# Six gate tiles of an encoder layer as two by two block products with seven blocks (Strassen), on one core

## The chip, the cores and the metric

The kernel runs on one core of a Trainium2 chip. The metric is the device time of one execution in microseconds (us). Before the change it is 935.38 us, the median of 3 runs (935.34 to 936.16 us). The profile is one execution, and TensorE was granted its full clock in it from 6.5 us to 931.5 us.

## What is computed

One layer of an encoder on 512 tokens of width 1024: three token mixers side by side (neighbourhood attention, grouped-query attention, attention to 256 memory tokens), each projected and weighted by a gate, then an output projection, a layer norm, a mixture of 16 experts in which each expert picks its 64 tokens, and a second layer norm.

```python
z = jnp.einsum('bsd,df->bsf', x, w_in[l])
q_na, k_na, v_na, q_g, k_g, v_g, q_m, gate_logits = jnp.split(z, _split_points(), axis=-1)
...
branches = jnp.stack([y_na, y_gqa, y_mem], axis=2)
proj = jnp.einsum('bsgk,gkd->bsgd', branches, w_branch[l])
gates = jax.nn.sigmoid(gate_logits + b_gate[l]).reshape(B, S, N_BRANCH, D)
merged = jnp.sum(gates * proj, axis=2)
mix = jnp.einsum('bsd,de->bse', merged, w_out[l])
x = layer_norm(DN_ALPHA * x + mix, ln1_g[l], ln1_b[l])
ffn = expert_choice_ffn(x, w_router[l], w_gate_up[l], w_down[l])
x = layer_norm(DN_ALPHA * x + ffn, ln2_g[l], ln2_b[l])
```

The gates are the part that the change touches: `gate_logits` has 3 x 1024 columns, 24 tiles of 128, eight for each branch.

## The kernel before

**Products in three passes.** Ahead of the experts every float32 operand is split into two parts of the type fp32r. `hi_lo` does this: a cast on ScalarE (`hi`), then a subtraction on VectorE (`lo`). A product is hi·hi + hi·lo + lo·hi, three instructions of TensorE (L306 to L308). The layer's input stands in SBUF as `xh` and `xl`, each in two halves (`a`, `b`) of 4 chunks x 512 tokens.

**Weight units.** The weights ahead of the experts are 74 units of 512 KB (128 x 1024), which `Stream` loads on SyncE's queue (L194), in two places `raw` by turns, and splits two units ahead of their use. A unit of a gate is 8 chunks of 128 columns: `gate_piece` takes one unit and makes 8 x 3 products of 128x512 into one PSUM bank of `mm` (3 banks), and ScalarE evacuates it with a tanh. Units 36 and 37 are the first two gate tiles of branch 1, unit 38 is the weight of its first projection, and 54 to 61 are the eight gate tiles of branch 0.

**Order.** Each engine carries out its instructions in the order in which the program gives them. Memory attention comes first, then the queries, keys and values of the second branch, `g_branch(2)` (gates and projections of the third input), the values of the neighbourhood attention (`g_na_v`), the bias table of its first two heads (`na_bias(0)`: 16 loads on SyncE and 6 sums on GpSimd), its queries and keys (`g_na_qk(0)`), and `g_branch(1)`, whose steps alternate with units of neighbourhood attention (`at.step`). In `between(jp)` the next two heads' bias, queries and keys follow. Then `g_na_gates` makes the eight gate tiles of branch 0, `g_na_proj` projects them, the output projection (`wo`) and the router follow, and the experts end the kernel. Small pieces of work (`bg`) are given out one at each step.

**The experts' weights.** They are 192 units of 1 MB (`gu` and `dn`), streamed by `Ring` through 24 places. The places are SBUF tiles which the mixers used before; `RING` is the order in which they are filled, `ring.more(7)` gives out the first loads behind certain weight units (`after`), and from the experts on each unit that has been read makes room for the next. The products of the experts are L1384 and L1433.

## Time and profile before

| what | value |
|---|---|
| median of 3 runs | 935.38 us |
| the profiled execution | 935.73 us |
| its span, first to last instruction | 934.0 us |
| TensorE busy | 917.7 us, 98% |
| VectorE busy | 452.5 us, 48% |
| ScalarE busy | 280.9 us, 30% |
| GpSimd busy | 71.9 us, 8% |
| queue 1 of the DMAs | 250.22 MB, 67.0% of 16 engines' span |

Times in the rows count from the span's start. PE is TensorE, PEld its weight loads, DVE VectorE, ACT ScalarE, POOL GpSimd, SP SyncE (its DMA queue is SPq). Products are pipelined: the second number of a row of TensorE is longer than the pace, and the pace is read from the distances of the starts. A row names the line, the operation, the tile written and those read, the shapes and how many instructions it stands for; behind it, in brackets, is the idle time of the engine before it and what ended it.

### The profile page before, as it was taken

How to read it: one execution, taken by the hardware profiler on the slowest of the kernel's cores; microseconds unless marked ns; L12 is line 12 of the kernel's file. 1: busy time of each engine (PE TensorE's matmuls, PEld its weight loads, DVE VectorE, ACT ScalarE, POOL GpSimd, SP SyncE). 2: the span in 40 equal slices, each digit the busy share in tenths (PEclk: the TensorE clock that was granted, in tenths of full speed). 3: DMA queues.
4: the chain of work that ended last, by engine and by line, in shares of the span. 5: the costliest groups of instructions: out<-in, count | busy, mean ns of one | idle time of the engine just before them, and what ended most of it. 6: DMA issues, size and time to landing. Idle time of an engine off the chain costs nothing.

```text
span 934.0 us, 13436 instructions
## 1 busy us (share of the span) xinstructions
PE 917.7 (98%) x5501; PEld 604.7 (65%) x5501; DVE 452.5 (48%) x858; ACT 280.9 (30%) x572; POOL 71.9 (8%) x107
## 2 busy tenths in 40 slices
PE   9999999999999999999999999999999999999996
PEld 8899988888888888888787344444343444543332
DVE  6447869875375576326445147223141323422246
ACT  6334443644344454334333011101011011301021
POOL 0100000000122230107023000000000000000001
PEclk9999999999999999999999999999999999999999
DMA  9322221221333332574879999999999999999996
GB/s 366 103 76 64 82 68 46 69 76 60 96 84 115 106 85 72 181 279 176 318 313 360 415 426 432 428 441 425 434 432 433 425 430 429 429 433 428 431 425 275
DMA packets 39868, 251.42 MB, mean 269 GB/s; under 512 B 12704, under 2 KB 13248, under 8 KB 24576
## 3 DMA queue, kind: packets, MB, share of 16 engines
q1 hardware_dynamic: 39584, 250.22, 67.0%
q8 instruction: 43, 0.70, 0.3%
q0 software_dynamic: 80, 0.26, 0.1%
q14 instruction: 17, 0.14, 0.0%
q10 hardware_dynamic: 144, 0.10, 0.0%
HBM read 247.42 MB, written 2.36 MB: 267 GB/s over the span
## 4 chain that ended last, share of the span: by engine, by line
PE 72%; DMA 20%; DVE 4%; ACT 2%; issue 1%; SPq 0%; POOLq 0%; POOL 0%; DVEq 0%; ACTq 0%
DMA dn<-in_wst 11%; DMA gu<-in_wst 8%; PE g L1384 7%; PE u L1384 6%; PE y L1433 6%; PE gate L306 5%; PE gate L308 4%; PE gate L307 4%; PE pr L306 2%; PE pr L307 2%; PE pr L308 2%; PE ga L1350 2%; PE gy L691 2%; PE nqk L308 2%; PE nqk L307 2%; PE nqk L306 2%
## 5 line engine op out<-in xcount | busy, mean ns | idle before, releaser
L1384 PE MATMUL g<-gu,xs 128*64 128x512 f32 x408 | 106.0, 598 | 1.1 <-DMA gu<-in_wst 1.0
L1384 PE MATMUL u<-gu,xs 128*64 128x512 f32 x408 | 104.9, 592 | 0.0
L1433 PE MATMUL y<-dn,hT 128*64 128x512 f32 x376 | 83.6, 593 | 0.9 <-DMA dn<-in_wst 0.8
L150 DVE TENSOR_TENSOR y<-y,y 64x512 fp32r<-64x512 f32 x28 | 19.3, 688 | 120.2 <-ACT y L149 120.2
L150 DVE TENSOR_TENSOR lo_twin<-raw_twin,whi 128x1024 fp32r<-128x1024 f32 x40 | 49.5, 1238 | 45.8 <-ACT whi L149 45.7
L149 ACT CAST y<-y 64x512 fp32r<-64x512 f32 x28 | 16.2, 580 | 174.1 <-PE y L1433 146.6
L1384 PEld LDWEIGHTS u<-gu,xs 128*64 128x64 f32 x408 | 29.4, 137 | 58.1 <-issue 57.6
L149 ACT CAST whi<-raw_twin 128x1024 fp32r<-128x1024 f32 x60 | 63.0, 1050 | 12.1 <-PE wo L1159 9.5
L1433 PEld LDWEIGHTS y<-dn,hT 128*64 128x64 f32 x376 | 27.0, 137 | 54.5 <-issue 51.2
L1384 PEld LDWEIGHTS g<-gu,xs 128*64 128x64 f32 x408 | 26.8, 137 | 46.6 <-issue 39.4
L1417 DVE COPY hT<-ht 128x512 f32<-128x512 f32 x15 | 10.4, 692 | 61.3 <-PE ht L1414 61.3
L306 PE MATMUL gate<-xha,whi 128*128 128x512 f32 x96 | 38.7, 403 | 0.0
L307 PE MATMUL gate<-xla,whi 128*128 128x512 f32 x96 | 37.4, 390 | 0.0
L306 PE MATMUL gate<-xhb,whi 128*128 128x512 f32 x96 | 37.3, 389 | 0.0
L307 PE MATMUL gate<-xlb,whi 128*128 128x512 f32 x96 | 37.3, 389 | 0.0
L712 POOL TENSOR_TENSOR bm<-bf,hm 128x256 f32<-128x256 f32 x24 | 17.9, 785 | 235.4 <-DMA bf<-in_rpb 231.5
L1521 DVE TENSOR_TENSOR acc<-acc,cb 128x512 f32<-128x512 f32 x56 | 34.0, 681 | 3.7 <-PE cb L1519 3.7
L1350 PEld LDWEIGHTS <-x 128*128 128x128 f16 (+1 forms) x576 | 29.7, 100 | 9.0 <-issue 8.7
L1405 DVE SCALAR_TENSOR_TENSOR h<-h,g 128x512 f32<-128x512 f32 x16 | 11.0, 687 | 50.0 <-ACT h L1404 50.0
L665 ACT ACTIVATE P_twin<-gs,nm 128x512 f32<-128x512 f32 x32 | 21.7, 684 | 42.8 <-DVE nm L664 42.8
L150 DVE TENSOR_TENSOR wlo<-raw_twin,whi 128x1024 fp32r<-128x1024 f32 x20 | 25.2, 1258 | 18.0 <-ACT whi L149 17.9
L308 PE MATMUL gate<-xha,lo_twin 128*128 128x512 f32 x80 | 31.2, 391 | 0.0
(481 smaller groups left out, 2000.5 us busy)
## 6 DMA issues: line engine op xcount, KB each, us to landing
gu<-in_wst SPq DMA_DIRECT2D x31, 2048.0 KB
gu<-in_wst SPq DMA_DIRECT2D x45, 1024.0 KB
raw_twin<-in_wu SPq DMA_DIRECT2D x65, 512.0 KB
dn<-in_wst SPq DMA_DIRECT2D x15, 2048.0 KB
dn<-in_wst SPq DMA_DIRECT2D x16, 1024.0 KB
gu<-in_wst SPq DMA_DIRECT2D x4, 4096.0 KB
dn<-in_wst SPq DMA_DIRECT2D x4, 4096.0 KB
gu<-in_wst SPq DMA_DIRECT2D x2, 3072.0 KB
```

Of the source, the lines that this page charges most:

```text
L149: nc.scalar.copy(hi, src)
L150: nc.vector.tensor_tensor(lo, src, hi.bitcast(F32), op=ALU.subtract)
L306: nc.tensor.matmul(acc, w_h, rh[:, k], start=(k == 0), stop=False)
L307: nc.tensor.matmul(acc, w_h, rl[:, k], start=False, stop=False)
L308: nc.tensor.matmul(acc, w_l, rh[:, k], start=False, stop=(k == nk - 1))
L665: nc.scalar.activation(self.p[:, h], self.s[h], AF.Exp, bias=nm[:, h:h + 1], accum_out=self.sm[:, h:h + 1])
L691: nc.tensor.matmul(self.y[h * 64:h * 64 + 64, j * P:(j + 1) * P], ST["vg"][:, kc, kvh * 64:kvh * 64 + 64], u.pt[:, h, kc], start=(kc == 0) ...
L712: nc.gpsimd.tensor_tensor(bm[:, h, ty].rearrange("p (b r c) -> p r b c", b=4, r=8), bf[:, h, :, 16 - 8 * ty:48 - 8 * ty].rearrange("p r (b ...
L1350: nc.tensor.matmul(g[r], part(i, m)[:, f * P + r.start:f * P + r.stop], oh[:, m], start=(i == 0 and m == 0), stop=(i == 1 and m == NT - 1))
L1384: nc.tensor.matmul(GU[e][b][hf * 64:hf * 64 + 64], xs, w[b][:, hf * 512:hf * 512 + 512], start=(k == 0), stop=(k == KD - 1))
L1433: nc.tensor.matmul(ys[o][o * 64:o * 64 + 64], hT[:, c, hf * 64:hf * 64 + 64], w[j][:, o * 512:(o + 1) * 512], start=(first and k == 0 and ...
L1521: nc.vector.tensor_tensor(a, a, cb, op=ALU.add)
```

## The change

Of the eight gate tiles of branch 0 the first two stay as they are. The other six are made as three couples. A couple's weights are a two by two matrix of blocks (two tiles, two halves of the inner dimension) and the input another (two halves of the inner dimension, two halves of the tokens); the product is made of seven block products and sums, each block being 4 chunks x 3 products of 128x256. The sums of the input's quarters (t1 to t4) are made once: x is loaded a second time (`load_x_again`), GpSimd subtracts (`mix_sum`, `mix_raw`), ScalarE casts and GpSimd subtracts the low halves (`mix_split`); t4 goes into a quarter of `xh` and `xl` (`mix_last`). Each couple's weights are summed on GpSimd and VectorE, and four of their sums or blocks are split (`Couple`). `g_couple` makes the seven blocks in two PSUM banks, with copies of the first results on ScalarE and sums on VectorE and GpSimd. The order of the places in the ring is another one, the first expert loads go out two units later, `router_scale` is given out in two parts and, with the rest of the router's preparation, nine steps later, `na_bias` of the next heads stands ahead of the attention steps, and the gates' results lie in other tiles.

```diff
-RING = ("E0", "A2", "A3", "A0", "A1", "B0", "B1", "A8", "P", "PT", "A4", "raw", "VS", "A5", "A6", "G0a", "G0b", "G1a", "lo", "X",
+RING = ("P", "PT", "B1", "E0", "A4", "A2", "A3", "A0", "B0", "A1", "A5", "A6", "A8", "VS", "raw", "G0a", "G0b", "G1a", "lo", "X",
...
-WIDTHS = ((0, 1), (N_SINGLE, 2), (N_PAIR, 4), (112, 2), (182, 1))
+WIDTHS = ((0, 1), (N_SINGLE, 2), (N_PAIR, 4), (112, 2), (181, 1))
...
+COUPLES = range(56, 62, 2)
...
+            self.stop = self.limit = COUPLES[0]
...
+            elif i - i % 2 in COUPLES[::2]:
+                if i % 2 == 0:
+                    self.wide = R("B1", [P, 2, 1024], f"raw{i}")
                 t = self.wide[:, i % 2]
...
-            while self.ns < min(N_UNITS, self.used + n):
+            while self.ns < min(self.stop, self.used + n):
                 self._split()
-            while self.nd < min(N_UNITS, self.ns + self.AHEAD_DMA):
+            self.ahead()
+
+        def ahead(self):
+            while self.nd < min(self.limit, self.ns + self.AHEAD_DMA):
...
+    def quarter(t, c):
+        return t[:, :, c * 256:c * 256 + 256]
+    mixed = {}
+    xq = []
+    def load_x_again():
+        for h in range(2):
+            xq.append(R(("A5", "A6")[h], [P, 4, S], f"xq{h}"))
+            nc.sync.dma_start(xq[h], xt[:, 4 * h:4 * h + 4])
+    def mix_sum(*which):
+        x11, x12, x21, x22 = (quarter(xq[h], c) for h in range(2) for c in range(2))
+        if 1 in which:
+            t12 = R("A7", [P, 2, 4, 256], "mix12")
+            mixed["sums"] = {1: t12[:, 0], 2: t12[:, 1], 3: x12}
+        t = mixed["sums"]
+        for i, a, b in ((1, x12, x11), (2, x22, t[1]), (3, x22, x12)):
+            if i in which:
+                nc.gpsimd.tensor_tensor(t[i], a, b, op=ALU.subtract)
+    def mix_split(*which):
+        for i in which:
+            t = mixed["sums"][i]
+            both = R(("E0", "A4", "A7")[i - 1], [P, 2, 4, 256], f"mx{i}", F32R)
+            mixed[f"t{i}"] = both[:, 0], both[:, 1]
+            nc.scalar.copy(both[:, 0], t)
+            nc.gpsimd.tensor_tensor(both[:, 1], t, both[:, 0].bitcast(F32), op=ALU.subtract)
+    def mix_raw():
+        ST["kept"] = R("A1", [P, 2048], "kept")
+        t4 = ST["kept"][:, :1024].rearrange("p (k c) -> p k c", k=4)
+        x21 = [quarter(x.t[1], 0).bitcast(F32) for x in (xh, xl)]
+        t2 = [t.bitcast(F32) for t in mixed["t2"]]
+        nc.gpsimd.tensor_tensor(t4, x21[0], t2[0], op=ALU.subtract)
+        nc.gpsimd.tensor_tensor(t4, t4, x21[1], op=ALU.add)
+        nc.gpsimd.tensor_tensor(t4, t4, t2[1], op=ALU.subtract)
+        mixed["raw4"] = t4
+    def mix_last():
+        mixed["t4"] = quarter(xh.t[0], 1), quarter(xl.t[0], 1)
+        hi_lo(*mixed["t4"], mixed.pop("raw4"))
+        mixed["x11"] = quarter(xh.t[0], 0), quarter(xl.t[0], 0)
+        for c in range(2):
+            mixed[f"x2{c + 1}"] = quarter(xh.t[1], c), quarter(xl.t[1], c)
+    class Couple:
+        def __init__(self, p):
+            self.p = p
+            ws.ahead()
+            i = COUPLES[p]
+            self.a, self.b = (ws.raw.pop(j).rearrange("p (h c) -> p h c", h=2) for j in (i, i + 1))
+            self.cells = {}
+            self.sums = ST["kept"][:, 1024:].rearrange("p (h c) -> p h c", h=2)
+        def cell(self, n, src):
+            i = "acb".index(n)
+            if self.p % 2 == 0:
+                both = R(("A2", "A0", "A3")[i], [P, 2, 1024], f"whl{self.p}{n}", F32R)
+                hl = both[:, 0], both[:, 1]
+            else:
+                lo = R("lo2", [P, 1024], f"wlo{self.p}{n}", F32R) if i == 2 else twins["lo"][0][:, i]
+                hl = R(("hi", "hiB", "hi3")[i], [P, 1024], f"whi{self.p}{n}", F32R), lo
+            hi_lo(*hl, src.rearrange("p h c -> p (h c)"))
+            self.cells[n] = hl
+        def sums_pool(self):
+            a, b, t = self.a, self.b, self.sums
+            (nc.gpsimd if self.p else nc.vector).tensor_tensor(t[:, 0], b[:, 0], b[:, 1], op=ALU.add)
+            nc.gpsimd.tensor_tensor(b[:, 0], a[:, 0], b[:, 0], op=ALU.subtract)
+        def first(self):
+            self.cell("a", self.a)
+            nc.vector.tensor_tensor(self.sums[:, 1], self.sums[:, 0], self.a[:, 0], op=ALU.subtract)
+        def second(self):
+            self.cell("c", self.sums)
+        def third(self):
+            self.cell("b", self.b)
+        def last_sum(self):
+            nc.vector.tensor_tensor(self.a[:, 1], self.a[:, 1], self.sums[:, 1], op=ALU.subtract)
+        def fourth(self):
+            self.cells["d"] = tuple(ST["rest"][:, self.p % 2, i] for i in range(2))
+            hi_lo(*self.cells["d"], self.a[:, 1])
+    def block(acc, cell, half, x, first=False, last=False):
+        wh, wl = (w[:, half * 512:half * 512 + 512].rearrange("p (k c) -> p k c", k=4) for w in cell)
+        th, tl = mixed[x]
+        for k in range(4):
+            nc.tensor.matmul(acc, wh[:, k], th[:, k], start=first and k == 0, stop=False)
+            nc.tensor.matmul(acc, wh[:, k], tl[:, k], start=False, stop=False)
+            nc.tensor.matmul(acc, wl[:, k], th[:, k], start=False, stop=last and k == 3)
+    def g_couple(name, c, nxt, evx, evy):
+        cells = c.cells
+        x, y = (PB("mm", f"{name}{i}") for i in "xy")
+        x0, x1, y0, y1 = x[:, :256], x[:, 256:], y[:, :256], y[:, 256:]
+        xs, ys = ST["kept"][:, :512], ST["kept"][:, 512:1024]
+        nxt(0)
+        block(x0, cells["a"], 0, "x11", first=True)
+        block(x1, cells["c"], 0, "t1", last=True)
+        nc.scalar.copy(xs, x)
+        c.fourth()
+        nxt(1)
+        block(y0, cells["c"], 1, "t2", first=True)
+        block(y1, cells["b"], 1, "t4", last=True)
+        nc.scalar.copy(ys, y)
+        for eng, i, j in ((nc.vector, ys[:, :256], xs[:, :256]), (nc.vector, xs[:, 256:], ys[:, :256]),
+                          (nc.gpsimd, ys[:, 256:], ys[:, :256])):
+            eng.tensor_tensor(i, i, j, op=ALU.add)
+        nxt(2)
+        yield
+        block(x0, cells["a"], 1, "x21", first=True)
+        block(x1, cells["d"], 0, "x22", last=True)
+        nc.vector.tensor_tensor(x, x, xs, op=ALU.add)
+        evx(x)
+        block(y0, cells["b"], 0, "t3", first=True, last=True)
+        nc.vector.tensor_tensor(y1, y0, xs[:, 256:], op=ALU.add)
+        nc.vector.tensor_tensor(y0, y0, ys[:, 256:], op=ALU.add)
+        nxt(3)
+        evy(y)
+        nxt(4)
+        yield
...
+                if (g, j) == (1, 7):
+                    mix_raw()
...
     def g_na_gates():
-        sg = [R("A4", [P, 4, S], "sg0"), R("A7", [P, 4, S], "sg1")]
-        ST["sg"] = sg
-        for j in range(8):
-            ev = gate_piece(0, j, sg[j // 4][:, j % 4])
+        sg = ST["sg"] = []
+
+        def place(j):
+            def f():
+                if j % 4 == 0:
+                    sg.append(R(("A8", "VS")[j // 4], [P, 4, S], f"sg{j // 4}"))
+                return sg[j // 4][:, j % 4]
+            return f
+
+        c, ws.limit = None, N_UNITS
+        for j in range(2):
+            ev = gate_piece(0, j, place(j))
+            if j == 0:
+                c = Couple(0)
+                c.sums_pool()
+                c.first()
+            else:
+                c.second()
+                c.third()
             yield
             ev()
+        mix_last()
+        ST["rest"] = R("B0", [P, 2, 2, 512], "rest", F32R)
+        c.last_sum()
+        for p in range(3):
+            ws.ns = ws.used = COUPLES[p] + 2
+            if p < 2:
+                n = Couple(p + 1)
+                nxt = [n.sums_pool, n.first, n.second, n.third, n.last_sum]
+            else:
+                ws.stop = N_UNITS
+                nxt = [lambda n=n: ws.prefetch(n) for n in (0, 1, 1, 2, 2)]
+            yield from g_couple(f"gate0{p}", c, lambda i: nxt[i](), *(gate_out(0, j, place(j)) for j in (2 * p + 2, 2 * p + 3)))
+            c = n
...
-        after[N_UNITS - 14 + i] = [lambda: ring.more(7)]
+        after[N_UNITS - 12 + i] = [lambda: ring.more(7)]
...
+    load_x_again()
     na_bias(0)
+    mix_sum(1, 2, 3)
     run(g_na_qk(0))
+    mix_split(1, 2)
     at.add([NaUnit(0, i) for i in range(2)])
-    ST["y0"] = (R("A5", [P, 4, S], "ynh", F32R), R("A6", [P, 4, S], "ynl", F32R))
     def between(jp):
+        if jp < 3:
+            na_bias(jp + 1)
+        if jp == 0:
+            mix_split(3)
+            ST["y0"] = (R("A5", [P, 4, S], "ynh", F32R), R("A6", [P, 4, S], "ynl", F32R))
         while at.units:
             at.step()
         if jp < 3:
-            na_bias(jp + 1)
             yield from g_na_qk(jp + 1)
             at.add([NaUnit(jp + 1, i) for i in range(2)])
...
-        wps.append(PB("mm", "wps")[:, :2 * NEXP])
+        wps.append(PB("S", "wps")[:, :2 * NEXP])
...
-    bg.extend([lambda: None, router_scale, lambda: None, router_sums, router_centre, ln_split])
+    bg.extend([lambda: None] * 9 + [lambda: router_scale(0), lambda: router_scale(1), lambda: None, router_sums, router_centre, ln_split])
```

## Rows read from the trace of the kernel before

**Rows 1.** Stretches: busy time by engine, clock, DMA share, GB/s
```profile
core 0: us, PE busy (x) PEld busy (x) DVE busy (x) ACT busy (x) POOL busy (x), PEclk, DMA share, GB/s
...
500.00:510.00 10.00, 9.79 (x116) 6.07 (x116) 3.25 (x15) 1.87 (x6) 1.13 (x4) 1.00 0.88 342
...
520.00:720.00 200.00, 199.71 (x1148) 83.06 (x1146) 68.65 (x130) 23.73 (x44) 0.00 (x0) 1.00 1.01 431
...
790.00:917.00 127.00, 121.70 (x688) 50.63 (x685) 43.15 (x99) 24.62 (x51) 0.00 (x0) 1.00 1.01 429
```

**Rows 2.** Chain that ended last: start us, us, what
```profile
504.40 1.08 PE g L1384 x4
...
720.94 30.73 DMA dn<-in_wst
```

**Rows 3.** Timeline of SyncE at the start of the experts: start us, us, what
```profile
506.38 4.66 SPq L898 DMA_DIRECT2D dn<-in_wst  x3
```

**Rows 4.** Timeline of TensorE: a gate tile (512 columns), a memory key (256 columns)
```profile
389.15 0.39 PE L308 MATMUL gate<-xha,lo_twin 128*128 128x512 f32 x1
...
393.23 0.39 PE L308 MATMUL gate<-xhb,lo_twin 128*128 128x512 f32 x1
...
15.21 0.28 PE L308 MATMUL mk<-firsth,wlo 128*128 128x256 f32 x1
...
19.53 0.28 PE L308 MATMUL mk<-firsth,lo_twin 128*128 128x256 f32 x1
```

**Rows 5.** Timeline of SyncE: the loads of the first bias table
```profile
240.71 10.78 SPq L706 DMA_DIRECT2D bf<-in_rpb  x16
```

**Rows 6.** Timeline of GpSimd, 250 us to 285 us
```profile
253.51 5.23 POOL L712 TENSOR_TENSOR bm<-bf,hm 128x256 f32<-128x256 f32 x6 [225.76 <-DMA bf<-in_rpb]
269.55 1.29 POOL L546 TENSOR_TENSOR macca<-macca,tm 128x512 f32<-128x512 f32 x1 [10.81 <-DVE tm L545]
275.31 2.21 POOL L546 TENSOR_TENSOR macca<-macca,tm 128x512 f32<-128x512 f32 x1 [4.46 <-DVE tm L545]
281.42 4.25 POOL L712 TENSOR_TENSOR bm<-bf,hm 128x256 f32<-128x256 f32 x6 [3.90 <-PE nt L762]
```

**Rows 7.** Timeline of ScalarE, 250 us to 270 us
```profile
255.19 1.06 ACT L149 CAST whi<-raw_twin 128x1024 fp32r<-128x1024 f32 x1 [0.93 <-DMA raw_twin<-in_wu]
256.27 0.69 ACT L514 ACTIVATE th<-gate,hm 128x512 f32<-128x512 f32 x1
```

**Rows 8.** Timeline of VectorE, 250 us to 270 us
```profile
256.28 1.85 DVE L150 TENSOR_TENSOR wlo<-raw_twin,whi 128x1024 fp32r<-128x1024 f32 x1 [0.59 <-ACT whi L149]
...
262.24 0.69 DVE L744 TENSOR_TENSOR P_twin<-ns,bm 128x512 f32<-128x512 f32 x1 [2.43 <-PE ns L736]
...
266.35 1.14 DVE L755 TENSOR_SCALAR P_twin<-P_twin,rc 128x256 f32<-128x256 f32 x4
```

**Rows 9.** Timeline of TensorE: a projection of branch 1, transposes of the first unit
```profile
262.56 0.39 PE L308 MATMUL pr<-ygh,wlo 128*128 128x512 f32 x1
...
268.52 1.03 PE L762 MATMUL nt<-ident,P_twin 128*128 128x128 f32 x8
```

**Rows 10.** Groups by line, 382.4 us to 415.5 us: busy us, mean ns, idle before
```profile
L150 DVE TENSOR_TENSOR lo_twin<-raw_twin,whi 128x1024 fp32r<-128x1024 f32 x4 | 4.9, 1225 | 12.6 <-ACT whi L149 12.6
...
L149 ACT CAST whi<-raw_twin 128x1024 fp32r<-128x1024 f32 x6 | 6.3, 1042 | 0.0
```

**Rows 11.** Stretches, columns as in rows 1: between early loads and experts
```profile
480.00:490.00 10.00, 9.92 (x78) 8.82 (x77) 7.00 (x30) 7.00 (x15) 3.32 (x5) 1.00 0.51 200
```

**Rows 12.** Stretches at the end; timeline of TensorE at two other places
```profile
927.80:931.50 3.70, 0.06 (x1) 0.00 (x0) 1.70 (x3) 0.00 (x0) 1.75 (x2) 1.00 0.01 2
931.50:934.00 2.50, 0.00 (x0) 0.00 (x0) 0.00 (x0) 0.00 (x0) 0.00 (x0) 0.50 0.26 105
...
1.35 4.21 PE L280 MATMUL warm<-ident 128*128 128x128 f32 x18 [1.35 <-POOL ident masks.py:199]
...
6.87 0.28 PE L331 MATMUL mk<-firstl,firsth 128*128 128x256 f32 x1
...
494.05 6.64 PE L1210 MATMUL warm<-ident 128*128 128x128 f32 x58
```

More of the change, by code (lines that the diff above doesn't have):

```diff
@@ L509, in gate_piece, with gate_out @@
+    def gate_out(g, j, dst):
+        return lambda acc: nc.scalar.activation(dst(), acc, AF.Tanh, bias=bg_t[:, g * 8 + j:g * 8 + j + 1], scale=0.5)
     def gate_piece(g, j, dst):
```

15 lines of the change are left out of this document (9 added, 6 removed).

## Prediction

> **What bounds the kernel now.** I read the view by stretches first, because a mean over the span mixes stages. From 520 us to 720 us the DMA share is 1.01 at 431 GB/s while TensorE is busy for 199.71 of 200 us; from 790 us to 917 us the share is still 1.01, and now TensorE is idle for 5.3 of 127 us [rows 1]. So the expert stage ends with its weight stream. The chain of waits says the same: the first expert product stands on it at 504.40 us, and from 720.94 us on it is the stream's DMAs [rows 2].
>
> When does that stream start to run full? All 24 places of the ring are taken before the experts begin, and a place comes free only when an expert product has read it: the queue's next load of `dn` goes out at 506.38 us [rows 3], about 2 us after the first product, and the share is 0.88 in the ten microseconds around it [rows 1]. From there the remaining 168 of 192 loads, 176 MB, need 410 us at 430 GB/s, which is 916 us, where the full stretch ends. **A shift of the first expert product is therefore a shift of the end, one for one, earlier or later.** TensorE work saved inside the expert stage would be worth nothing, but the change saves ahead of it. In that part, 380 us to 504 us, TensorE sets the pace: gate products follow each other with no gap.
>
> **The products.** Four rows give the pitches: products of 512 columns run from 389.15 to 393.23 us in 18 steps, 0.2267 us each; products of 256 columns, with another weight tile each time, from 15.21 to 19.53 us in 36 steps, 0.120 us each [rows 4]. Two gate tiles are now 2 x 24 x 0.2267 = 10.88 us. A couple is seven blocks of 12 products: 84 x 0.120 = 10.08 us. Three couples save 3 x 0.80 = **2.40 us**, far less than an eighth of 32.6 us, because a product of half the columns costs more than half. The two products of `router_sums` only move from the gates to the projections, where TensorE is also the bound: nothing gained.
>
> **The hold in front of the third branch.** The changed program copies t1 and t2 on ScalarE (`mix_split(1, 2)`) right behind the evacuations of `g_na_qk(0)`, and both are made by GpSimd, behind the six bias sums of `na_bias(0)`. Engines work in program order, so I follow the times.
> - SyncE now issues the two loads of x before the 16 of the bias table, which take 10.78 us, 0.67 us each [rows 5]; two more are 0.9 to 1.3 us. The bias sums then start not at 253.51 but near 254.6 us. They take 4.25 us with VectorE quiet and 5.23 us beside it [rows 6]; VectorE will be held too, so 4.25: 258.9 us.
> - Subtractions of 128x1024 on GpSimd aren't in the trace. The nearest row is 128x512 at 1.29 us alone and 2.21 us beside a VectorE subtraction [rows 6]: 2.58 us to 4.42 us. I take 2.58, as VectorE has nothing to do here. t1 is ready at 261.4 us, t2 at 264.0 us.
> - ScalarE copies t2 in 1.05 us (the casts of that size [rows 7, 10]): 265.1 us. Queued behind it are the cast of the weight unit at 255.19 us, unit 38 of the first projection of branch 1, then the tanh of the gate at 256.27 us [rows 7], then the next cast. Unit 38's cast now ends at 266.2 us.
> - VectorE's subtraction for its low half took 1.85 us with GpSimd at work beside it [rows 8] and 1.225 us in the mean where it wasn't [rows 10]. GpSimd is at work until about 272 us (t3 and the low halves of t1 and t2), so 1.85: 268.0 us. The projection's third product, which needs that half, began at 262.56 us [rows 9]. TensorE stands still for 5.4 us (4.8 with 1.225).
> - Behind it the softmax of the first neighbourhood unit is late as well. VectorE takes it up after the next unit's subtraction, at 269.8 us instead of 262.24 us; from there to the end of its normalising it was 267.49 - 262.24 = 5.25 us [rows 8], so 275.1 us. The transposes that need it went out at 268.52 us [rows 9]. That path is the later one (TensorE alone would be there by 268.0 + 22 x 0.2267 and the next scores, about 274 us): 6.6 us late, 5.7 us with undisturbed subtractions.
> TensorE had no gap here in the profile of before, so nothing later takes this back. I take **6.0 us**, with 5.3 and 7.0 us as ends.
>
> **The rest of the sums and casts.** `mix_split(3)` and the third sum fall in places where ScalarE and GpSimd wait anyway; y0 is first written behind the products of the first units, after them: nothing, and 1.05 us if its copy met a softmax. `mix_raw` puts three subtractions (7.7 us at 2.58) on GpSimd from 367 us; their result is needed some 20 us later. It can slow the last softmax, 0 to 1 us; I take 0. Within the couples ScalarE has 3 casts of 1.04 us, a half cast, two copies and two tanh, about 6.4 us of 10.1; VectorE 3 subtractions of 1.225 us and the smaller sums, about 8.2 us of 10.1. In the gate stage of before there were 6 casts of 1042 ns in 33 us and VectorE sat idle 12.6 us before 4 of its subtractions [rows 10]. The engines keep up, with one to two microseconds in hand, and weights are cast one couple ahead. `mix_last` overwrites part of `xh` between the last whole gate tile and the first block: if the first block waits for the whole of it, 3.7 us are lost; if only for the quarters it reads, none. I take **0.5 us** for all this, ends 0 and 4 us.
>
> **Loads and router.** The seven early expert loads go out two units later, and the ring's order puts the place `raw` further back. What hides them: the DMAs are half idle (0.51) between 480 and 490 us, after the early loads and before the experts [rows 11]. If that cover were gone, a load of 1.05 MB would cost 2.4 us at 430 GB/s. Router scaling (under 2 us of VectorE) goes into the projections, and its result is needed only in the output projection, a stage later. Both: nothing. Moving `na_bias` ahead of the attention steps passes no load and no GpSimd instruction: nothing.
>
> **The sum.** 935.73 - 2.40 + 6.0 + 0.5 = 939.8 us for the profiled execution, which was 0.35 us above the median of three, so **939.5 us** against 935.38. The ends of the terms give 938.3 to 944 us; the likeliest case's own range is 938 to 942 us.
>
> **The rivals.**
> - *The clock falls in the hold.* Behind the last products of the kernel the granted clock stayed at 1.00 (2.4 GHz) while TensorE had next to nothing to do, and was 0.50 (1.2 GHz) from 931.50 us [rows 12], 3.7 us after the last product. The hold is longer, 5.4 us. At the start 18 products of 128 columns took 4.21 us, twice the pace of the 58 in 6.64 us later, and full pace is seen at 6.87 us, 5.5 us after the first [rows 12]. Half of 5.5 us is lost: 2.7 us, less about 1 us for which the softmax is late anyway: 941.2 to 942.2 us. Against it: one standstill may be too short, or fall unluckily. Chance 0.21. The Trainium skill, "TensorE: Matmul & The Clock Gate", section "HAM oscillation — how this bites in real kernels", says that idle gaps make the gate throttle again and that work after each gap starts cold; by that rule the result is this rival's rather than the forecast's. No run here shows it inside a kernel.
> - *The hold doesn't reach TensorE*, and the kernel is faster. That is so if both halves of unit 38 are there by 262.56 us, which needs t2 by about 259 us, that is the sums of x ahead of the bias sums: x, 2 MB, takes 5 us at 430 GB/s from its issue near 241 us, so GpSimd could do them from about 248 us if it didn't stand at the bias table. Then 935.38 - 2.40 + 0.3 = 933.3 us. Against it stands the program order of GpSimd: the sums come after `na_bias(0)`. Chance 0.13.
> - *The hold is half as long*, because a subtraction of 128x1024 on GpSimd costs little over 1.3 us: t2 at 261.5 us, all later times 2.5 us earlier, and the end is 937.0 us less the 0.5: about 936.5 us, within 0.2%. Against it: both kinds of GpSimd rows give 2.5 ns or more for an element [rows 6]. Chance 0.10.
> - *The couples aren't shorter than the tiles*: casts and sums of VectorE come late, or each block waits for its copies, and a couple takes 10.9 us as before. Then 942 us. The pitch of rows 4 and the idle time of rows 10 speak against it. Chance 0.06.
>
> **How the numbers follow.** Forecast 0.50, clock 0.21, longer couples 0.06: slower by over 0.2% (1.87 us, about what a measurement of this kernel can tell from no change) 0.77. Half hold: within 0.2%, 0.10. No hold: faster, 0.13. The range leaves out the no-hold case and the far ends of the couples: 934.8 to 943.0 us.
>
> **What would show it.** Right: on ScalarE a wait for GpSimd of 8 us or more between 254 and 265 us, TensorE idle for about 5 us before the third product of the first `pr` of branch 1, an idle gap before its transposes, six gates' work in about 30.3 us, the first expert product near 508 us, and from there an unchanged stage of about 410 us. Wrong: no idle time of TensorE at 262 us; a couple of over 10.5 us; a gap at the first block (`mix_last`); or a DMA share under 1 after 515 us, which would mean that the early loads mattered.

## The result and the profile after

The changed kernel takes 945.59 us (median of 4 runs, 945.03 to 946.17) against 935.36 us (934.97 to 936.16) in the same sitting: a ratio of 1.0113 [1.0101, 1.0126], 10.2 us longer. The forecast was 939.5 us and its range ended at 943.0 us: the sign was right, the size was not, and the time lies outside the range. The profiled execution has a span of 943.9 us, 9.95 us over that of before, and this difference is what the traces have to explain.

The way to read such a difference is to look up the same six points in both traces and to take the time from each to the next. The points are TensorE's first query product of the neighbourhood branch (239.38 us in the trace of before), the first one of the second head pair (269.31), the first of the last value products (380.55), the first projection of branch 0 (415.49), the first expert product (504.40 [rows 2]) and the end (933.95). The table shows by how much each stage is longer or shorter than before, in us, for the changed kernel and for the kernels of the experiments below:

| kernel | start | first softmax | to the last values | gates of branch 0 | projection to experts | experts | sum | median |
|---|---|---|---|---|---|---|---|---|
| stage of before | 239.38 | 29.93 | 111.24 | 34.94 | 88.91 | 429.55 | 933.95 | 935.36 |
| the change | +0.47 | **+8.83** | **+1.75** | **-2.20** | **+2.38** | -1.29 | +9.95 | 945.59 |
| a1, sums first | +0.82 | +0.10 | +1.75 | -2.06 | +2.35 | -1.44 | +1.51 | 937.35 |
| a3, long filling | +0.52 | +10.05 | +1.75 | -2.05 | +2.33 | -0.79 | +11.81 | 947.03 |
| a3b, short filling | -0.16 | +9.09 | +1.77 | -1.77 | +2.36 | -1.31 | +9.98 | 946.44 |
| a3c, low parts later | +0.44 | +8.01 | +8.52 | -1.42 | +2.37 | -1.05 | +16.87 | 950.75 |
| a4, one router item | +0.74 | +8.49 | +1.79 | -2.27 | +1.65 | -1.56 | +8.84 | 945.52 |
| b1, raw sums alone | -0.13 | 0.00 | +1.78 | 0.00 | -0.01 | -0.77 | +0.88 | 936.79 |
| b2, delay alone | +0.79 | 0.00 | 0.00 | 0.00 | +9.44 | -0.07 | +10.15 | 945.23 |
| c5, raw sums late | -0.13 | 0.00 | 0.00 | +2.55 | +2.18 | -0.93 | +3.67 | 939.77 |
| c8, last loads wide | -0.25 | 0.00 | +1.79 | -2.17 | +2.30 | -0.84 | +0.83 | 937.76 |
| c9, router early | -0.33 | 0.00 | +1.75 | -1.93 | +0.29 | -0.96 | -1.18 | 934.95 |
| d1, raw sums early | +0.32 | +0.51 | +0.05 | -2.71 | +2.36 | -0.88 | -0.35 | 934.82 |
| d2, d1 and c9 | +0.16 | +0.46 | +0.01 | -2.49 | +0.29 | -0.66 | -2.23 | 932.51 |

The columns come from one profiled execution each and scatter in the start (-0.33 to +0.82) and in the expert stage; the medians are of 4 to 10 runs. In c5 the gap described below lies behind the first of the last value products, and so it counts in its column of the gates. So the change costs time at three places and gains at one; what is left are the start and the expert stage.

**Stretches of the changed kernel** (columns as in [rows 1]):

```profile
262.50:265.60 3.10, 0.22 (x2) 0.01 (x1) 0.00 (x0) 1.04 (x1) 3.02 (x2) 1.00 0.00 0
265.60:272.40 6.80, 3.79 (x8) 2.58 (x9) 3.64 (x2) 3.61 (x4) 6.80 (x4) 0.50 0.21 67
...
510.00:520.00 10.00, 9.55 (x120) 6.88 (x120) 4.19 (x18) 1.40 (x5) 2.13 (x5) 1.00 0.86 339
530.00:730.00 200.00, 199.71 (x1156) 83.63 (x1154) 69.14 (x133) 23.73 (x44) 0.00 (x0) 1.00 1.01 431
800.00:927.00 127.00, 122.25 (x693) 50.74 (x687) 43.33 (x99) 24.62 (x51) 0.00 (x0) 1.00 1.01 429
393.50:424.34 30.84, 30.65 (x254) 30.42 (x253) 23.88 (x31) 16.82 (x24) 8.82 (x7) 1.00 0.40 147
```

The last three groups of columns of a line are clock, DMA share and GB/s. TensorE stands still until 268.47 us, for 5.75 us (timeline below). Meanwhile its clock falls from 1.00 (2.4 GHz) to 0.50 (1.2 GHz), where it stays from 265.6 to 272.4 us, although products run again in the last 3.9 us of that. GpSimd is busy for 9.82 of the 9.90 us. The expert stretches are like those of [rows 1], read ten microseconds later. The three couples, 393.50 to 424.34 us, keep TensorE busy for 30.65 of 30.84 us.

**The chain of waits of the changed kernel**, from the bias table to the second head pair and at two later places (start us, us, what; "issue" is time in which nothing that the profile shows was waited for):

```profile
255.06 2.12 DMA bf<-in_rpb
...
257.43 4.22 POOL bm L882 x6
261.66 2.31 POOL mix L538
...
264.05 2.35 POOL mix L538
...
267.38 1.04 ACT whi L150
...
269.13 0.94 ACT whi L150
...
270.13 2.99 issue
...
381.30 3.87 DVE P_twin L925 x2
...
385.21 0.98 PE nt L932 x6
```

The first seven pieces are the hold that the prediction described, link by link: bias loads, bias sums, t1 and t2 on GpSimd, then the weight casts of ScalarE, then VectorE. The 2.99 us called "issue" are a single VectorE subtraction, as the next view shows. The last two are a place to which the prediction gave nothing.

**Timelines of the changed kernel around these places** (start us, us, engine, line, operation, tiles, forms, count, in brackets the idle time before it and its releaser); SyncE, GpSimd, ScalarE, VectorE, TensorE in this order:

```profile
241.18 1.85 SPq L528 DMA_DIRECT2D xq<-in_xt  x2
243.08 12.57 SPq L876 DMA_DIRECT2D bf<-in_rpb  x16
...
257.43 4.22 POOL L882 TENSOR_TENSOR bm<-bf,hm 128x256 f32<-128x256 f32 x6 [229.25 <-DMA bf<-in_rpb]
...
268.65 6.69 POOL L546 TENSOR_TENSOR mx<-mix,mx 128x1024 fp32r<-128x1024 f32 x2
...
380.16 2.40 POOL L554 TENSOR_TENSOR kept<-kept,xlb 128x1024 f32<-128x1024 f32 x1
382.64 2.37 POOL L555 TENSOR_TENSOR kept<-kept,mx 128x1024 f32<-128x1024 f32 x1
...
264.00 1.04 ACT L545 CAST mx<-mix 128x1024 fp32r<-128x1024 f32 x1 [9.28 <-POOL mix L538]
266.42 1.04 ACT L545 CAST mx<-mix 128x1024 fp32r<-128x1024 f32 x1 [1.38 <-POOL mix L538]
267.38 1.04 ACT L150 CAST whi<-raw_twin 128x1024 fp32r<-128x1024 f32 x1
...
268.45 1.33 DVE L151 TENSOR_TENSOR wlo<-raw_twin,whi 128x1024 fp32r<-128x1024 f32 x1 [12.29 <-ACT whi L150]
270.09 3.00 DVE L151 TENSOR_TENSOR lo_twin<-raw_twin,whi 128x1024 fp32r<-128x1024 f32 x1 [0.31 <-ACT whi L150]
273.12 0.69 DVE L914 TENSOR_TENSOR P_twin<-ns,bm 128x512 f32<-128x512 f32 x1
...
381.30 4.38 DVE L925 TENSOR_SCALAR P_twin<-P_twin,rc 128x256 f32<-128x256 f32 x4
...
448.22 0.42 DVE L151 TENSOR_TENSOR lnhl<-rt,lnhl 32x128 fp32r<-32x128 f32 x1
448.68 0.69 DVE L1194 SCALAR_TENSOR_TENSOR tm<-sg,pr 128x512 f32<-128x512 f32 x1
...
268.47 0.80 PE L315 MATMUL pr<-ygh,whi 128*128 128x512 f32 x1 [5.75 <-ACT whi L150]
...
277.63 1.23 PE L932 MATMUL nt<-ident,P_twin 128*128 128x128 f32 x8 [0.36 <-DVE P_twin L925]
...
385.21 0.98 PE L932 MATMUL nt<-ident,P_twin 128*128 128x128 f32 x6 [1.42 <-DVE P_twin L925]
...
449.42 0.50 PE L1335 MATMUL wo<-whi,mhl 128*128 128x512 f32 x1 [1.50 <-DVE tm L1194]
```

Three things are to be seen. At 264 us ScalarE waits 9.28 us for GpSimd with the cast of unit 38 queued behind, and TensorE waits 5.75 us for that cast. At 381.30 us VectorE's four scalings, 1.14 us in [rows 8], take 4.38 us, and TensorE waits 1.42 us for them; GpSimd's raw sums lie beside them. One by one the four take 1.42, 2.52, 0.34 and 0.34 us: the first ends 0.15 us after GpSimd's second raw sum, the second 0.15 us after its third, and the other two run alone. At 449.42 us the output projection waits 1.50 us for an evacuation of VectorE that stands behind the low half of a weight unit and the last router item. Before the change TensorE had none of these three waits.

### The profile page after: what moved, and what is told of

The parts are those of the page before. It is cut to its first block, busy times and chain, and to the rows that moved or that the text cites. A ratio compares the mean times of both kernels' runs of the same rounds, so it can differ in the third digit from the quotient of the medians.

```text
span 943.9 us, 13726 instructions
## 1 busy us (share of the span) xinstructions
PE 918.3 (97%) x5609; PEld 610.3 (65%) x5609; DVE 481.8 (51%) x887; ACT 292.5 (31%) x588; POOL 104.1 (11%) x124
## 3 DMA queue, kind: packets, MB, share of 16 engines
HBM read 249.52 MB, written 2.36 MB: 267 GB/s over the span
## 4 chain that ended last, share of the span: by engine, by line
PE 66%; DMA 20%; DVE 6%; ACT 3%; issue 2%; POOL 1%; SPq 1%; POOLq 0%; DVEq 0%; ACTq 0%
DMA gu<-in_wst 18%; PE g L1562 7%; PE u L1562 7%; PE y L1611 6%; PE gate L315 3%; PE gate L317 3%; PE gate L316 3%; PE ga L1528 2%; PE gy L861 2%; PE gt L846 1%; PE pr L315 1%; PE gq L332 1%; PE gq L330 1%; PE gq L331 1%; PE pr L316 1%
## 5 line engine op out<-in xcount | busy, mean ns | idle before, releaser
L150 ACT CAST whi<-raw_twin 128x1024 fp32r<-128x1024 f32 x54 | 56.7, 1050 | 11.0 <-PE wo L1337 8.7
L151 DVE TENSOR_TENSOR wlo<-raw_twin,whi 128x1024 fp32r<-128x1024 f32 x18 | 23.0, 1277 | 22.7 <-ACT whi L150 22.6
L315 PE MATMUL gate<-xha,whi 128*128 128x512 f32 x72 | 29.2, 405 | 0.0
L1582 ACT ACTIVATE h<-g 128x512 f32<-128x512 f32 x16 | 9.6, 597 | 62.0 <-PE g L1562 59.7
L917 ACT ACTIVATE P_twin<-P_twin,nm 128x256 f32<-128x256 f32 x32 | 16.0, 502 | 40.1 <-DVE nm L915 40.1
L316 PE MATMUL gate<-xla,whi 128*128 128x512 f32 x72 | 28.1, 390 | 0.0
```

What stands on the lines that cost most here:

```text
L150: nc.scalar.copy(hi, src)
L151: nc.vector.tensor_tensor(lo, src, hi.bitcast(F32), op=ALU.subtract)
L315: nc.tensor.matmul(acc, w_h, rh[:, k], start=(k == 0), stop=False)
L316: nc.tensor.matmul(acc, w_h, rl[:, k], start=False, stop=False)
```

## The experiments

Names in the table are short for the runs; a, c and d are edits of the changed kernel (c and d with several at a time), b edits of the kernel before. The theory after the first reading of the traces: three separate waits (scaled sums, raw sums, router) and a fall of the clock inside the first, worth 2.2 us, add up; whatever delays the first expert product delays the end.

**a1: the scaled sums ahead of the bias sums.**
```diff
     load_x_again()
-    na_bias(0)
     mix_sum(1, 2, 3)
+    na_bias(0)
```


> The changed kernel with the three GpSimd sums of x ahead of the first bias sums instead of behind them; nothing else. Theory (ScalarE's copies wait for GpSimd in program order, the projection's weights wait behind them, and the clock falls in the standstill): x lands near 248 us, t2 is there near 256 us, the copies end near 257 us, TensorE has no gap at 262 us, the clock stays at 1.00, and the whole 8.8 us that the changed kernel had lost between the first query product and the next one are gone: 945.6 - 8.8 = 936.8 us. Rival (the loss is not the order but GpSimd's work itself, which slows VectorE beside it): the gap shrinks by less than half, 942 us or more.


Measured: 937.35 us, ratio 1.0023 [1.0013, 1.0033]. The 8.83 us of the first softmax go to 0.10 us, the rest of the ledger stays. The stretch in which the changed kernel stood still (columns as above):

```profile
262.50:268.40 5.90, 5.90 (x30) 4.94 (x30) 4.60 (x7) 2.52 (x10) 5.90 (x3) 1.00 0.57 176
```

The timeline of GpSimd in the same run:

```profile
247.75 2.40 POOL L538 TENSOR_TENSOR mix<-xq 128x1024 f32<-128x1024 f32 x1 [220.32 <-DMA xq<-in_xt]
...
258.12 5.21 POOL L882 TENSOR_TENSOR bm<-bf,hm 128x256 f32<-128x256 f32 x6 [2.27 <-DMA bf<-in_rpb]
```

GpSimd makes t1 from 247.75 us on, while it would otherwise wait for the bias table, and TensorE waits for nothing: it is busy for the whole 5.90 us at clock 1.00. The order of two calls was 8.2 of the 10.2 us.

**a3: idle products in the standstill, too many.** Between the first softmax's scores and the first projection, 45 calls of a product that computes nothing used:
```diff
+                if (g, j) == (1, 0):
+                    hold = PB("Y", "warmh")
+                    for _ in range(45):
+                        nc.tensor.matmul(hold[:, :P], ident, ident, start=True, stop=True)
                 acc = proj_piece(u, jj, *ST[f"y{g}"], f"pr{g}{j}")
```


> The changed kernel with 45 idle products of 128 columns ahead of the first projection of branch 1, about 5.2 us of TensorE work that nobody reads, in the time in which TensorE stood still. Theory (of the 8.8 us lost here some 6.4 are the wait and the rest is the clock at 0.50 until 272.4 us): the wait for the cast stays, the clock stays at 1.00, the second projection follows 2.75 us behind the first as before, and the time is 945.6 - 2.3 = 943.3 us. Rival (the softmax behind it would have been late anyway, so the clock cost nothing): 945.6 us and a longer gap before the transposes.


Measured: 947.03 us, ratio 1.0123 [1.0106, 1.0140]. A call turned out to be two product rows, so the filling took 10.21 us, twice what was meant, and itself held the projection (first product at 272.57 us). The clock stayed at 1.00, but the run can't price it: inconclusive.

**a3b: the same with 23 calls, 5.30 us.**


> The changed kernel with 46 idle product rows (23 calls of two rows, about 5.3 us at the full clock) put on TensorE between the first product of branch 1 and the second, in the place where TensorE stood still while the scaled sums held up the cast of unit 38. The idle rows compute nothing that is used. The earlier run with 90 such rows kept the clock at 1.0 but filled 10.2 us, about 4 us more than the standstill. Theory (the standstill of about 6 us lies on TensorE's path and the fall of the clock after it costs about 2.2 us more): the clock stays at 1.0 through 262 to 275, the second product follows the first 2.85 us later in place of 4.97, the end comes 1.5 to 2.5 us earlier than in the changed kernel, so 943.1 to 944.1. Rival (the norm of the second product's operand sets the pace behind the standstill, the clock is hidden in it): the query and key products of branch 1 start where they did, 945 to 946.


Measured: 946.44 us, ratio 1.0129 [1.0112, 1.0145]. The stretch of the filling:

```profile
262.00:268.00 6.00, 5.23 (x47) 5.04 (x46) 0.00 (x0) 3.03 (x3) 5.92 (x3) 1.00 0.01 3
```

Timelines of VectorE and TensorE behind it:

```profile
269.69 3.03 DVE L151 TENSOR_TENSOR lo_twin<-raw_twin,whi 128x1024 fp32r<-128x1024 f32 x1 [0.30 <-ACT whi L150]
...
277.26 1.23 PE L936 MATMUL nt<-ident,P_twin 128*128 128x128 f32 x8 [1.35 <-DVE P_twin L929]
```

The clock stays at 1.00, the second projection comes 3.8 us behind the first in place of 5.0, and nothing is won (+9.09 us in the stage, +8.83 in the change): the transposes now wait 1.35 us for the softmax where they had waited 0.36 us. My theory fell and the rival held: **the clock fell, but its price was hidden**. What is last behind the standstill is VectorE's queue: two low halves (1.35 and 3.03 us) stand ahead of the softmax.

**a3c: the low halves of t1 and t2, on GpSimd at 268.65 us, put behind the first gate step; the short filling stays.**
```diff
-            nc.gpsimd.tensor_tensor(both[:, 1], t, both[:, 0].bitcast(F32), op=ALU.subtract)
+            low = lambda t=t, both=both: nc.gpsimd.tensor_tensor(both[:, 1], t, both[:, 0].bitcast(F32), op=ALU.subtract)
+            lows.append(low) if i < 3 else low()
...
     def between(jp):
+        while lows:
+            lows.pop(0)()
```


> The changed kernel with 46 idle product rows in the standstill, as the earlier run that gave 946.44, and GpSimd's two low parts of the scaled sums (3.3 us each) issued behind the first gate step's bias sums in place of beside the standstill's end. Theory (with the clock kept at 1.0, what sets the pace behind the standstill is VectorE's queue: two low parts of weights, one of them drawn out to 3.0 us beside GpSimd, stand ahead of the softmax): the low part takes 1.2 us again, the wait of 1.35 us ahead of the transposes goes to about 0 and the query and key products of branch 1 start 1.2 to 1.4 us earlier after the stage's begin than in that run (37.7 us behind the first ones in place of 39.0); time 944.6 to 945.6. Rival (the clock sets the pace): no change against that run, 946 to 947.


Measured: 950.75 us, ratio 1.0160 [1.0144, 1.0176]. The stage in question did as the theory says: the low half takes 1.22 us in place of 3.03, and the second head pair starts 37.9 us after the first products in place of 39.0. But the edit made a new hold of the same kind 25 us later, which I had not looked for. The stretch behind that hold:

```profile
292.30:299.10 6.80, 5.71 (x13) 4.03 (x14) 4.72 (x4) 4.75 (x8) 6.57 (x6) 0.50 0.28 80
```

Timelines of VectorE, ScalarE and TensorE:

```profile
271.00 1.22 DVE L151 TENSOR_TENSOR lo_twin<-raw_twin,whi 128x1024 fp32r<-128x1024 f32 x1 [0.31 <-ACT whi L150]
...
291.29 1.04 ACT L545 CAST mx<-xq 128x1024 fp32r<-128x1024 f32 x1 [7.57 <-POOL mx L546]
292.24 1.04 ACT L150 CAST whi<-raw_twin 128x1024 fp32r<-128x1024 f32 x1
...
293.33 0.80 PE L315 MATMUL gate<-xha,whi 128*128 128x512 f32 x1 [3.56 <-ACT whi L150]
```

The copy of t3 takes the buffer in which the sums t1 and t2 lie, so on ScalarE it waits 7.57 us for the moved subtractions, with a weight cast behind it. Here the fall of the clock is not hidden. Ten products, from the third one behind the gap (294.61 us) to 299.04 us, take 4.43 us where 10 x 0.2267 is 2.27, so by an estimate from these rows some 2.2 us go to the clock. With the gap of 3.56 us that is most of the 6.8 us by which the column exceeds that of the change.

**b1: the raw sums alone, in the kernel before.** Three GpSimd operations of 128x1024 at the place where the changed kernel has them; nothing reads what they write.
```diff
                 yield
+                if (g, j) == (1, 7):
+                    ...
+                    nc.gpsimd.tensor_tensor(kept, q[0], q[1], op=ALU.subtract)
+                    nc.gpsimd.tensor_tensor(kept, kept, q[2], op=ALU.add)
+                    nc.gpsimd.tensor_tensor(kept, kept, q[3], op=ALU.subtract)
```


> The kernel before, with three GpSimd subtractions and additions of 128x1024 alone put where the changed kernel has the raw sums of the couples (ahead of the last accumulation of the second gate step); what they write is used by nothing. Theory (beside such operations VectorE's four scaled copies take 4.4 us in place of 1.14, and TensorE waits for them): the group of four at 372 takes 4.2 to 4.5 us, a gap of about 1.4 us ahead of the transposes at 374 appears, and the time is 1.4 to 2.0 us longer, 936.6 to 937.3. Rival (the prediction's step: these sums hide beside the gate products, at most 0.3 us): no gap, 935.0 to 935.7.


Measured: 936.79 us, ratio 1.0017 [1.0008, 1.0026]. Timelines of VectorE and TensorE:

```profile
371.88 4.38 DVE L761 TENSOR_SCALAR P_twin<-P_twin,rc 128x256 f32<-128x256 f32 x4
...
375.79 0.98 PE L768 MATMUL nt<-ident,P_twin 128*128 128x128 f32 x6 [1.42 <-DVE P_twin L761]
```

The same 4.38 us and the same gap of 1.42 us as in the changed kernel, with no other part of the change in it. The stage is 1.78 us longer, the median 1.55 us.

**c5: the raw sums behind the last accumulation** (a1's order, and couple 0's last difference on VectorE).
```diff
-                if (g, j) == (1, 7):
-                    mix_raw()
...
                     nc.gpsimd.tensor_tensor(macc[:, j], macc[:, j], tmp, op=ALU.add)
+                if (g, j) == (1, 7):
+                    mix_raw()
...
-            nc.gpsimd.tensor_tensor(b[:, 0], a[:, 0], b[:, 0], op=ALU.subtract)
+            (nc.gpsimd if self.p else nc.vector).tensor_tensor(b[:, 0], a[:, 0], b[:, 0], op=ALU.subtract)
```


> Scaled sums issued ahead of the bias sums (as in the run that gave 937.35), and in addition the raw sums of the couples (three GpSimd operations of about 2.4 us) issued behind the last accumulation of the second gate step in place of before it, with couple 0's last difference on VectorE so that its operand is not late. Theory (VectorE's four scaled copies at L925 take 4.4 us in place of 1.1 because GpSimd's raw sums run beside them, and TensorE waits 1.4 us for them): the four copies take about 1.1 us each group again, the gap of 1.4 us ahead of the transposes at 377 goes, and the end comes 1.4 to 1.8 us earlier, about 935.6 (935.2 to 936.2). Rival (the copies are slow for another reason, as the order of VectorE's own queue): the gap stays and the time is 937.0 to 937.6. A second rival: the raw sums now come too late for the couples, or slow another group of VectorE; then a gap stands at the head of the couples and the time is 937 to 940.


Measured: 939.77 us, ratio 1.0059 [1.0042, 1.0075]: the second rival. Timelines of VectorE and TensorE:

```profile
371.87 1.14 DVE L925 TENSOR_SCALAR P_twin<-P_twin,rc 128x256 f32<-128x256 f32 x4
...
375.55 2.77 DVE L588 TENSOR_TENSOR raw<-raw 128x512 f32<-128x512 f32 x1
378.24 3.41 DVE L151 TENSOR_TENSOR whl0a<-raw,whl0a 128x1024 fp32r<-128x1024 f32 x1
381.58 2.82 DVE L592 TENSOR_TENSOR kept<-kept,raw 128x512 f32<-128x512 f32 x1
384.32 0.68 DVE L936 COPY PT_twin<-nt 128x512 f32<-128x512 f32 x1
...
385.06 1.12 PE L954 MATMUL ny<-PT_twin,v_shift 128*64 128x128 f32 x8 [3.55 <-DVE PT_twin L936]
```

The scalings are at 1.14 us again and their gap is gone. The slowness has moved to the operations that now lie beside the raw sums (GpSimd is at these from 374.92 to 383.85 us), and the copy that the value products need stands behind these: a gap of 3.55 us in place of the 1.41 of a1. So the cause is right and the cure was wrong.

**d1: the raw sums 18 us earlier**, behind the bias sums of the fourth head pair, with a1's order. A free buffer for that long was had by letting the couples' common buffer and the couples' first weights change places (B1, A1), and the biases likewise (A8, B1):
```diff
-        ST["kept"] = R("A1", [P, 2048], "kept")
+        ST["kept"] = R("B1", [P, 2048], "kept")
...
         while at.units:
             at.step()
+        if jp == 2:
+            mix_raw()
```


> Scaled sums issued ahead of the bias sums, and the raw sums moved some 18 us ahead, right behind the bias sums of the fourth head pair, where VectorE has a free stretch (their buffer and the one of the couples' first weights change places to make this possible, and the biases change places among themselves). Theory (what counts is only which VectorE operations stand beside the three GpSimd operations): the four scaled copies at 372 take 1.1 us again, the gap of 1.4 us ahead of the transposes goes, the low parts at 354 to 357 take up to 3 us in place of 1.2 but wait for nobody, and the time is 1.0 to 1.7 us under 937.35, about 936.0. Rival (the low parts are late then, TensorE waits at 362, or the norm's operations behind them are): 937.0 to 939.0.


Measured: 934.82 us, ratio 0.9993 [0.9983, 1.0002]. The stage is +0.05 us in place of +1.75, the gap is gone, the time is 2.5 us under a1 (1.9 us in the profiled executions), more than the 1.0 to 1.7 us expected. The gates are 0.65 us shorter too and the first softmax 0.41 us longer, neither of which I had foreseen; no run takes the other moves of this edit apart.

**a4: one router item, the split, at the third step of the gates.**
```diff
-    bg.extend([lambda: None] * 9 + [lambda: router_scale(0), ..., router_centre, ln_split])
+    bg.extend([lambda: None] * 2 + [ln_split] + [lambda: None] * 6 + [lambda: router_scale(0), ..., router_centre])
```


> The changed kernel with the split of the layer norm's rows (the last of the router's preparations) given out at the third step of the gates instead of at the seventh step of the projections. Theory (this split stands on VectorE ahead of a projection's evacuation and waits there for ScalarE's casts, so that the output projection lacks a PSUM bank for 1.5 us at 449 us): the gap is gone, 945.6 - 1.5 = 944.1 us. Rival (the banks are late because of the router's scaling and sums as a whole, or of slower evacuations): the gap stays at over 1 us, 945.6 us.


Measured: 945.52 us, ratio 1.0110 [1.0093, 1.0127], no change in the time; in the trace the gap ahead of the output projection is 0.77 us in place of 1.50. Half right: the split is half of the wait; that the rest belongs to the other router items is shown by the next run, not by this one.

**c9: all router items from the second gate step on, with a1's order.**
```diff
-    bg.extend([lambda: None] * 9 + [lambda: router_scale(0), ...
+    bg.extend([lambda: None] + [lambda: router_scale(0), ...
```


> Scaled sums issued ahead of the bias sums, and the router's scaling, sums, centring and split handed out one step of the gate stage each from its second step on, in place of after nine empty steps. Theory (the last router item, the split, stands on VectorE ahead of the eviction that the output projection waits for, because it waits for ScalarE's casts): the gap of 1.5 us ahead of the projection at 441 goes, and the end comes 1.0 to 1.8 us earlier than 937.35, about 935.8. Rival (the router's work then meets the couples' combinations, which VectorE also makes): the couples take longer by what the gap gave, 937.0 to 938.5. Second rival (what is given back after the first expert product takes the gain): 937.0 to 937.6 though the first expert product starts earlier.


Measured: 934.95 us, ratio 0.9998 [0.9988, 1.0008]. No gap is left at the output projection, the stage is +0.29 us in place of +2.35, and the gates lose 0.13 us. It won 2.4 us against a1, where 1.0 to 1.8 were expected: the gap was 1.49 of the stage's 2.06 us, and the other 0.57 us lie in smaller shifts of the projections that no single wait shows.

**c8: the last expert loads as wide as before, with a1's order.**
```diff
-WIDTHS = ((0, 1), (N_SINGLE, 2), (N_PAIR, 4), (112, 2), (181, 1))
+WIDTHS = ((0, 1), (N_SINGLE, 2), (N_PAIR, 4), (112, 2), (182, 1))
```


> Scaled sums issued ahead of the bias sums, and the boundary from which the expert loads are issued singly put back from load 181 to 182, where the kernel before has it. Theory (the 1.3 us that the changed kernel gets back between its first expert product and its end come from the finer last loads): the stretch from the first expert product to the end grows by about 1.3 us to the 429.5 of the kernel before, and the time is about 938.6. Rival (they come from expert loads having landed earlier, whatever the width): no change, 937.0 to 937.7.


Measured: 937.76 us, ratio 1.0034 [1.0020, 1.0048]; the expert stage is 428.71 us long, not 429.55, and the time is within the scatter of a1's. The finer last loads are not what shortens that stage.

**b2: the kernel before with 88 idle product rows ahead of the first expert's gather.** 44 calls, again twice as long as meant.
```diff
+    keep_warm(44, "mm")
     onehot(0)
```


> The kernel before with 44 idle products (5.0 us) ahead of the first gather of the experts, so that the first expert product comes 5.0 us later and all else is the same. Theory of the prediction (a shift of the first expert product is a shift of the end, one for one): 935.4 + 5.0 = 940.4 us. Rival (part of a delay is given back by a stream that has got further, as the changed kernel ended 9.95 us later after a first product that came 11.23 us later): 935.4 + 3.7 to 4.4 = 939.1 to 939.8 us.


Measured: 945.23 us, ratio 1.0103 [1.0086, 1.0120]. The first expert product is 10.22 us later and the end 10.15 us: one for one, as the prediction has it. The timeline of TensorE:

```profile
514.62 1.08 PE L1384 MATMUL g<-gu,xs 128*64 128x512 f32 x4
```

**d2: sums first, raw sums early, router early.**


> The three moves together: scaled sums ahead of the bias sums, raw sums 18 us earlier, router work from the second step of the gate stage on. Theory (the three costs lie at three different places on one path and add): 934.95 less 1.0 to 1.7, so 933.2 to 934.0, faster than the kernel before by 1.2 to 2.1 us. Rival (what is won ahead of the experts is lost to their loads, which then land too late): 934.5 to 935.3.


Measured: 932.51 us (6 runs, 932.26 to 933.50), ratio 0.9970 [0.9958, 0.9982]: 2.7 us faster than the kernel before, 13.1 us faster than the change as it was made, and 0.7 us under the range that was expected. Timelines of GpSimd and VectorE:

```profile
350.81 2.39 POOL L553 TENSOR_TENSOR kept<-xhb,mx 128x1024 f32<-128x1024 f32 x1
...
356.70 3.41 DVE L151 TENSOR_TENSOR lo_twin<-raw_twin,whi 128x1024 fp32r<-128x1024 f32 x1
...
372.65 1.14 DVE L923 TENSOR_SCALAR P_twin<-P_twin,rc 128x256 f32<-128x256 f32 x4
```

Two stretches of it, around the last softmax and at the end of the gates:

```profile
372.00:382.00 10.00, 10.00 (x60) 8.22 (x61) 6.56 (x12) 4.98 (x8) 7.46 (x6) 1.00 0.33 134
391.00:413.63 22.63, 22.63 (x191) 22.63 (x190) 17.77 (x28) 12.60 (x20) 5.52 (x5) 1.00 0.52 198
```

The low half still takes 3.41 us beside the raw sums, but here nobody waits for it; TensorE is busy for all of 372 to 382 us and of the couples' last 22.63 us.

## Why the prediction was right or wrong

The mechanisms that bound the kernel and made the hold were right. Three terms of the sum failed: the hold was sized too small (6.0 us for 8.83), and two costs were put at nothing, the raw sums (1.55 us) and the moved router work (about 2.1 us).

- **What bounds the kernel: right.** The expert stretches show the same rates, and b2 shows the shift of the end one for one. In the change itself the first expert product came 11.23 us later and the end 9.95. What the shift leaves out: the expert stage of the profiled executions is between 428.0 and 428.9 us in the changed kernel and its variants, and 429.55, 429.48 and 428.78 us in the kernel before, b2 and b1. So it is about 0.5 to 1 us shorter with the changed order of loads, or it scatters by that much; c8 excludes the last loads' width, and the rest stays open.
- **The products, -2.40 us: right.** The gates are 2.20 us shorter, and 1.4 to 2.7 us in the other kernels where no new gap stands in them. The couples' rival (10.9 us each) falls: three take 30.84 us, 10.28 each, against 10.08 worked out.
- **The hold, +6.0 us: the mechanism was right, the size was not; 8.83 us.** The order of events was as written, but late from the first step: the bias sums start at 257.43 us, not near 254.6. The two loads of x took 1.85 us on SyncE, not 0.9 to 1.3, and the 16 loads of the table 12.57 us, not the 10.78 of [rows 5]. The bias sums (4.22 us for 4.25) and the subtractions of 128x1024 (2.34 to 2.36 us for 2.58) were right. At the end one low half took 3.00 us where 1.85 was taken from [rows 8]: two GpSimd operations of 3.3 us lay beside it, and no row of before shows a subtraction beside so much. The transposes went out at 277.63 us, 9.1 us later than in [rows 9], in place of 6.6.
- **The clock's rival: it happened, and cost nothing.** I left the fall of the clock out of the likeliest case and gave the rival 1.7 us more. The clock did fall, at 265.6 us, for 6.8 us. What failed is the rival's subtraction of 1 us for a softmax that is late anyway: the softmax was late enough to cover it all (a3b). The Trainium skill, "TensorE: Matmul & The Clock Gate", section "HAM oscillation — how this bites in real kernels", says that after an idle gap that is long enough the work starts cold. The traces agree for this gap and for those of 3.55 us in c5 and 3.56 us in a3c, not for those of 1.4 to 1.5 us. The price depended on who else was late: nothing here, some 2.2 us in a3c.
- **The raw sums, "0 to 1, take 0": wrong, 1.55 us (b1's median; 1.75 to 1.79 us in the stage).** I costed what GpSimd has to do and whether its result is late, and allowed at most 1 us for the last softmax, without a row for it. What failed is the size of the slowing: 1.14 us became 4.38, on the path to TensorE.
- **Loads and router, "both: nothing": wrong for the router, about 2.1 us (2.35 of a1 less 0.29 of c9), right for the early loads,** of which no wait shows. I asked when the result is needed and not what is queued behind the items on VectorE: there it was the evacuations which the output projection needs.
- **The rival "the hold doesn't reach TensorE"** (933.3 us) described a1's order of calls, which gives 937.35 us: it left out the same two costs. With both taken away as well, d2, it is 932.51 us.

By the ledger: 935.73 + 0.47 (start) + 8.83 - 2.20 + 1.75 + 2.38 - 1.29 = 945.67 us, the profiled execution's time, against 939.8 of the forecast's sum. Of the 5.8 us that were missing, 2.8 are the hold's size, 1.3 the raw sums less the 0.5 that stood for the rest, 2.4 the router's stage, 0.5 the start, 0.2 the couples, and 1.3 came back at the end.

## What to carry to other kernels

A step that is moved onto an idle engine has to be costed at two places: what waits behind the instruction that waits for it (here a weight cast behind a copy: 8.8 us for the order of two calls), and which operations of VectorE will lie beside it when the engine is GpSimd. Before an idle engine's work is called free, name for each of its stretches the VectorE operations there and who waits for them; put it beside operations with a PSUM operand or with time to spare. And a fall of the clock costs only what no other engine's delay covers (nothing in the change, some 2.2 us in a3c): price it against the next path, not alone.

## What the runs showed of the hardware

- Four scalings of 128x256 on VectorE, SBUF to SBUF: 1.14 us alone, 4.37 to 4.38 us beside GpSimd's additions of 128x1024 (the change, a1, b1, c9). A subtraction of 128x1024 with both operands in SBUF: 1.22 us alone, 2.2 to 3.4 us beside such work in most rows (3.00 in the change, 3.41 in c5 and d2). The times look like waits for whole operations of the other engine and not like a slower pace. The low half at 270.09 us of the change ends 1.1 us after GpSimd's first subtraction (268.65 to 272.00 us). The one before it, at 268.45 us, started ahead of that subtraction and took 1.33 us, and there GpSimd's took 3.35 us in place of 2.4. Beside the scalings GpSimd's raw sums kept their 2.40 and 2.37 us. No run tests shorter GpSimd operations.
- Beside the same GpSimd work VectorE's additions from PSUM stay at 0.69 us (the one at 273.12 us above). The Trainium skill, "Advanced Engine Details and Errata", section "VectorE Performance Modes", says that VectorE's second SBUF port is shared with GpSimd, so that GpSimd's instructions and those of VectorE's two-port modes block each other. The rows of the scalings agree and give the size; the subtractions are held up as well, and for these the section's table lists no two-port mode.
- The clock fell in these standstills of TensorE: in the change (5.75 us long; 5.39 us for the same one in a4), in c5 (3.55 us) and in a3c (3.56 us), each time while TensorE stood still, and it was still 0.50 after the products had begun again: in the change until 272.4 us, 3.9 us after the first. In the gaps of 1.4 to 1.5 us it stayed at 1.00.
- A product called with two fp32 operands of 128 columns shows as two product rows; 45 calls took 10.21 us.
